# Swapping the issuing engines of two first loads in a convolution with residual

## The chip, the cores and the metric

The kernel runs on one core of one Trainium2 chip. The metric is the device time of one execution in microseconds (us), as the median of several.

## The reference

A 3x3 convolution with zero padding over 16 images of 64 channels, 64 x 64 pixels, to 64 output channels, plus a residual of the output's shape, all in float32:

```python
x_pad = np.pad(x, ((0, 0), (0, 0), (1, 1), (1, 1)))
# for every b, co, ci, kh, kw:
output[b, co] += weight[co, ci, kh, kw] * x_pad[b, ci, kh:kh+64, kw:kw+64]
return output + residual
```

The images, the residual and the output are 16.78 MB each, the weights 0.15 MB: 50.48 MB pass between memory and core.

## The kernel before

Two images make a pair; a pair of images or of residuals is one tile of 128 partitions with rows of 16 KB (2.1 MB). ScalarE casts each image to bfloat16, TensorE (PE) convolves it in 24 matmuls, VectorE (DVE) adds the residual into the tile `ro`, which is then stored. The weights are transposed by PE once and cast by VectorE and ScalarE.

The loads and stores stand in SyncE's program, in order, and so in one queue. Only the first residual load is on ScalarE's queue:

```python
NXR = 3       # image tiles
NXP = 4       # cast images
...
for p in range(NPAIR):                       # on SyncE
    if p >= NXR:
        nc.sync.wait_ge(s_half, 2 * (p - NXR) + 3)     # ScalarE has freed the tile
    if p == 0:
        to_the_front(load_x(p))
        nc.sync.dma_start(out=wraw[:, :], in_=w_rows[:, :]).then_inc(s_w, 16)
    else:
        load_x(p)
    ...                                      # residual loads i = 1..6 follow their pairs
wait_ro(nc.sync, len(RES) - 2)
for pairs in EARLY:                          # stores of pairs 0-1, 2-3, 4-5, 6
    nc.sync.wait_ge(s_add, 2 * pairs.stop + 1)
    store(pairs).then_inc(s_out, 16)
...
to_the_front(load_ro(0, nc.scalar))          # on ScalarE
for n in range(B):
    ...
    if im == 0:
        nc.scalar.wait_ge(s_x[p % NXR], 16 * (p // NXR + 1))
    i = nc.scalar.copy(out=t[64:128, 0:J, :], in_=x4[hp, :, 0, :])
    ...
    if n >= NXP:
        i._wait_ge(s_conv, n - NXP + 1)      # PE has freed the cast image
    ...
    if n == 0:                               # ScalarE's share of the weight casts
        nc.scalar.wait_ge(s_id, NZERO + 1)
```

`to_the_front` moves an issue ahead of everything else that its engine does, so that it goes out within about 0.1 us of the start instead of at about 1 us. The last pair is stored after this program, in two halves.

## Time and profile before

| | before |
|---|---|
| time, median of 3 runs | 122.21 us (122.2 to 122.54) |
| span of the profiled execution | 120.6 us |
| bytes moved | 50.48 MB, 419 GB/s over the span |
| PE, DVE, ACT busy | 73%, 63%, 52% |
| first convolution matmul | 18.12 us |
| VectorE done, last stores issued | 108.6 us, 108.9 and 109.3 us |

### The profile page before, as it was taken

Reading aid. Unit: us, or ns where it says so; the run is one execution under the profiler, and the core shown is the slowest. Engines: PE = TensorE matmul, PEld = TensorE weight load, DVE = VectorE, ACT = ScalarE, POOL = GpSimd, SP = SyncE. Lnnn points to the kernel's source line nnn. Section 1 sums busy time; section 2 is a strip of 40 time slices with the busy share of each in tenths; the row PEclk is TensorE's granted clock in tenths of the full one; section 3 lists DMA queues with packets and bytes.
Section 4 is the critical chain, followed back from the end, with each engine's and each line's share of the span. In section 5 each row is a group of like instructions: output and inputs, shape, how many; then the busy total and the mean of one; then the engine's idle time right before and its main releaser. Section 6 shows DMA issues by size and latency. Waiting matters only on the chain.

```text
span 120.6 us, 734 instructions
## 1 busy us (share of the span) xinstructions
PE 87.7 (73%) x389; PEld 10.7 (9%) x105; DVE 76.0 (63%) x40; ACT 63.1 (52%) x37; POOL 2.4 (2%) x16
## 2 busy tenths in 40 slices
PE   0000609999999999999999999999999999400000
PEld 0000300111101110101010101010101010000000
DVE  0000080039898898988989898898988989890000
ACT  4001999999988595875959578595800000000000
POOL 5200000000000000000000000000000000000000
PEclk9999999999999999999999999999999999995555
DMA  7999999999999999999999999999999999999994
GB/s 239 429 424 429 430 429 429 429 435 435 435 429 429 424 429 424 429 435 424 435 429 435 435 435 418 421 459 435 429 429 429 429 429 435 435 435 429 399 427 168
DMA packets 3808, 50.48 MB, mean 419 GB/s; under 512 B 352, under 2 KB 480, under 8 KB 480
## 3 DMA queue, kind: packets, MB, share of 16 engines
q1 hardware_dynamic: 3664, 48.38, 94.2%
q10 hardware_dynamic: 144, 2.10, 4.1%
HBM read 33.70 MB, written 16.78 MB: 419 GB/s over the span
## 4 chain that ended last, share of the span: by engine, by line
PE 71%; DVEq 2%; DVE 2%; issue 0%
PE ps L101 54%; PE ps L100 17%; DVEq L142 2%; DVE ro L220 2%
## 5 line engine op out<-in xcount | busy, mean ns | idle before, releaser
L220 DVE TENSOR_TENSOR ro<-ps,ro 64x2048 f32<-64x2048 f32 x32 | 73.2, 2288 | 17.7 <-PE ps L101 17.2
L101 PE MATMUL ps<-xp,wl 128*128 128x504 bf16 (+1 forms) x288 | 80.0, 388 | 0.2
L190 ACT CAST xp<-xr 64x2048 bf16<-64x2048 f32 x16 | 30.3, 1896 | 22.5 <-PE ps L101 13.1
L100 PE MATMUL ps<-xp,wl 128*128 128x504 bf16 (+1 forms) x92 | 35.9, 390 | 3.4 <-PEq L241 3.4
L194 ACT CAST xp<-xr 64x2048 bf16<-64x2048 f32 x16 | 30.4, 1898 | 0.4
L100 PEld LDWEIGHTS ps<-xp,wl 128*128 128x128 bf16 x96 | 9.5, 99 | 79.1 <-issue 79.1
L206 DVE CAST wl<-ps 32x192 bf16<-32x192 f32 x8 | 2.8, 348 | 14.9 <-PE ps L233 14.8
L233 PE MATMUL ps<-ident,wraw 128*32 128x128 f32 x9 | 2.1, 412 | 12.6 <-DMA wraw<-in_weight_dram 12.6
L233 PEld LDWEIGHTS ps<-ident,wraw 128*32 128x32 f32 x9 | 1.2, 137 | 13.0 <-issue 12.6
L190 ACT ACT_TABLE_LOAD x1 | 1.3, 1283 | 1.1 <-SPq L142 1.1
L199 ACT CAST wl<-ps 32x192 bf16<-32x192 f32 x4 | 1.2, 306 | 0.0
L177 POOL MEMSET xp<- 64x64 bf16 x4 | 0.6, 146 | 0.2
L176 POOL MEMSET xp<- 64x64 bf16 x4 | 0.6, 144 | 0.2
L165 POOL TENSOR_SCALAR_AFFINE_SELECT ident<-ident 128x128 f32<-128x128 f32 x1 | 0.3, 292 | 0.2 <-POOL ident L163 0.2
L179 POOL MEMSET wl<- 64x192 bf16 x1 | 0.3, 253 | 0.1
L178 POOL MEMSET wl<- 64x192 bf16 x1 | 0.3, 251 | 0.1
L163 POOL MEMSET ident<- 128x128 f32 x1 | 0.2, 204 | 0.7 <-SPq L142 0.7
L277 POOL MEMSET const-bfloat16-1.0<- 128x1 bf16 x1 | 0.1, 111 | 0.0
L277 POOL MEMSET const-uint8-127<- 128x1 uint8 x1 | 0.1, 111 | 0.0
L277 POOL MEMSET const-float32-1.0<- 128x1 f32 x1 | 0.1, 108 | 0.0
L277 POOL MEMSET const-float32-0.0<- 128x1 f32 x1 | 0.1, 103 | 0.2 <-issue 0.2
## 6 DMA issues: line engine op xcount, KB each, us to landing
xr<-in_x_dram SPq DMA_DIRECT2D x8, 2048.0 KB, 14.4
out_dram<-ro SPq DMA_DIRECT2D x3, 4096.0 KB, 19.2
ro<-in_residual_dram SPq DMA_DIRECT2D x2, 4096.0 KB, 20.7
ro<-in_residual_dram SPq DMA_DIRECT2D x2, 2048.0 KB, 18.1
ro<-in_residual_dram ACTq DMA_DIRECT2D x1, 2048.0 KB, 12.0
ro<-in_residual_dram SPq DMA_DIRECT2D x2, 1024.0 KB, 18.8
out_dram<-ro SPq DMA_DIRECT2D x1, 2048.0 KB, 13.7
out_dram<-ro SPq DMA_DIRECT2D x2, 1024.0 KB, 9.4
```

The costliest lines, as they stand in the source:

```text
L100: return e.matmul(out=out_, lhsT=lhsT, rhs=rhs, start=start, stop=stop, skip_group_check=True)
L101: return e.add_instruction(mybir.InstMatmult(name=nc.get_next_instruction_name(), engine=PE, ins=[e.lower_ap(rhs), e.lower_ap(lhsT)], outs ...
L142: with tc.tile_critical(no_gpsimd_drain=True):
L176: nc.gpsimd.memset(t[0:64, 0, :], 0.0).then_inc(s_id, 1)
L177: nc.gpsimd.memset(t[64:128, J, :], 0.0).then_inc(s_id, 1)
L190: i = nc.scalar.copy(out=t[64:128, 0:J, :], in_=x4[hp, :, 0, :])
L194: nc.scalar.copy(out=t[0:64, 1 : J + 1, :], in_=x4[hp, :, 1, :]).then_inc(s_pack, 1)
L199: i = nc.scalar.copy(**weight_block(h, *b))
L206: i = nc.vector.tensor_copy(**weight_block(h, *b))
L220: i = nc.vector.tensor_tensor(out=o4[hp, :, par, :], in0=psj[64 * par : 64 * par + 64, :, :], in1=o4[hp, :, par, :], op=ADD)
L233: i = nc.tensor.transpose(out=tp[0:32, t // 3, 128 * (t % 3) : 128 * (t % 3) + 128], in_=wraw3[:, :, t], identity=ident[:, :])
L277: nc = _bacc.Bacc("TRN2", target_bir_lowering=False, num_devices=1)
```

## The change

The intent: the two first loads go out at the same time on two queues. The change swaps them, so that SyncE's front has the residual and ScalarE's front has the image that ScalarE itself waits for.

```diff
-    def load_x(p):
-        return nc.sync.dma_start(out=xr[p % NXR][:, :], ...
+    def load_x(p, e=nc.sync):
+        return e.dma_start(out=xr[p % NXR][:, :], ...
@@ SyncE
             if p == 0:
-                to_the_front(load_x(p))
+                to_the_front(load_ro(0, nc.sync))
                 nc.sync.dma_start(out=wraw[:, :], in_=w_rows[:, :]).then_inc(s_w, 16)
@@ ScalarE
-        to_the_front(load_ro(0, nc.scalar))
+        to_the_front(load_x(0, nc.scalar))
```

More of the change, by code (lines that the diff above doesn't have):

```diff
@@ L79 @@
     s_add = sem("s_add")
-    def load_x(p):
-        return nc.sync.dma_start(out=xr[p % NXR][:, :], in_=x_bc[128 * p : 128 * p + 128, :]).then_inc(s_x[p % NXR], 16)
+    def load_x(p, e=nc.sync):
+        return e.dma_start(out=xr[p % NXR][:, :], in_=x_bc[128 * p : 128 * p + 128, :]).then_inc(s_x[p % NXR], 16)
     def load_ro(i, e):
```

## The prediction

> **What bounds the kernel now.** I read the page's busy shares by slice first, because the change touches nothing but two loads at the front, and only a kernel that is bound there could feel it.
>
> ```profile
> PE   0000609999999999999999999999999999400000
> DVE  0000080039898898988989898898988989890000
> ACT  4001999999988595875959578595800000000000
> DMA  7999999999999999999999999999999999999994
> GB/s 239 429 424 429 430 429 429 429 435 435 435 429 429 424 429 424 429 435 424 435 429 435 435 435 418 421 459 435 429 429 429 429 429 435 435 435 429 399 427 168
> DMA packets 3808, 50.48 MB, mean 419 GB/s; under 512 B 352, under 2 KB 480, under 8 KB 480
> ```
>
> PE has gaps before its first convolution matmul and is done five slices before the end. The transfers have none: every slice but the first and the last is at 9, at some 430 GB/s. 50.48 MB at 430 GB/s is 117.4 us, and the span is 120.6 us. So the time is the length of one unbroken stream of transfers, plus a start and an end. Two stretches at each end, from the table of stretches (the last column is GB/s), give those:
>
> ```profile
> 0.00:1.00 1.00, 0.00 (x0) 0.00 (x0) 0.00 (x0) 0.00 (x0) 0.21 (x4) 1.00 0.00 0
> 1.00:2.00 1.00, 0.00 (x0) 0.00 (x0) 0.00 (x0) 0.93 (x1) 0.60 (x3) 1.00 1.08 262
> ...
> 118.00:119.00 1.00, 0.00 (x0) 0.00 (x0) 0.00 (x0) 0.00 (x0) 0.00 (x0) 0.50 0.74 311
> 119.00:120.60 1.60, 0.00 (x0) 0.00 (x0) 0.00 (x0) 0.00 (x0) 0.00 (x0) 0.50 0.00 0
> ```
>
> 262/430 of the second microsecond is filled, so data flows from about 1.4 us; 311/430 of the last but one, so it stops at about 118.7. That is 117.3 us of stream, 1.4 us before and 1.9 us after: the 120.6 us. The chain that ended last is put down to PE for 71%, but it is followed from an engine's last instruction at 108.6 us and does not see the queue of stores behind which the last one stands. I set it aside for this reason.
>
> Second, the front, by the timeline (start, length, then the instruction):
>
> ```profile
> 0.00 0.38 SPq L82 DMA_DIRECT2D xr<-in_x_dram  x1
> 0.12 0.36 ACTq L88 DMA_DIRECT2D ro<-in_residual_dram  x1
> 1.11 0.33 SPq L150 DMA_DIRECT2D wraw<-in_weight_dram  x1
> 1.50 0.56 SPq L82 DMA_DIRECT2D xr<-in_x_dram  x1
> ...
> 11.54 1.90 ACT L190 CAST xp<-xr 64x2048 bf16<-64x2048 f32 x1 [9.19 <-DMA xr<-in_x_dram]
> 12.61 2.08 PE L233 MATMUL ps<-ident,wraw 128*32 128x128 f32 x9 [12.61 <-DMA wraw<-in_weight_dram]
> 13.46 1.90 ACT L194 CAST xp<-xr 64x2048 bf16<-64x2048 f32 x1
> 14.80 2.89 DVE L206 CAST wl<-ps 32x192 bf16<-32x192 f32 x8 [14.80 <-PE ps L233]
> 15.27 1.26 ACT L199 CAST wl<-ps 32x192 bf16<-32x192 f32 x4
> ...
> 18.12 0.59 PE L100 MATMUL ps<-xp,wl 128*128 128x512 bf16 x1 [3.44 <-PEq L241]
> ```
>
> The landings of single issues, picked out of the trace by their start: the first image load lands 11.5 us after 0.00, the first residual load 12.0 us after 0.12 (so at 12.1), the weights 11.4 us after 1.11 (at 12.5). The first matmul at 18.12 waits for weights: they land, PE transposes until 14.7, VectorE casts until 14.80 + 2.89 = 17.69. ScalarE's branch, which hangs on the image, ends at 15.27 + 1.26 = 16.53. The image branch has 1.16 us of slack.
>
> **What the Trainium skill says.** "DMA: Bandwidth & Descriptors", section "Queues, rings and completion order": the two issuing engines each own a row of rings on the same 16 transfer engines, and each transfer engine goes round robin between rows, packet by packet. The trace agrees in outline: the two first loads, 4.19 MB together (9.8 us at 430 GB/s), were issued together and landed 0.6 us apart instead of one after the other. The same page, "Issuing engines are not separate DMA queues": issuing from several engines saves only the issue time; here 0.36 to 0.38 us per issue. Section "Where 436 GB/s comes from" gives 435.2 GB/s as the ceiling of the memory's ports; the slices sit at 424 to 435, with single ones at 459 that I take for packets counted at a slice's edge. So there is no rate left to win. "Perfetto Trace Analysis", section "Identifying the Most-Contended Engine", asks for utilization rather than occupancy for transfers, which is why I use GB/s here and not the digit 9.
>
> **The change part by part.** Nothing is added or removed: 2 issues swap queues, everything behind them keeps its place (PE, DVE and POOL have the same instructions; ACT and SP differ in their first one only). Both loads are 2.1 MB in 128 rows of 16 KB, so the bytes and packets on each queue do not change.
>
> 1. Bytes: 50.48 MB before and after. 0 us.
> 2. Start of the stream: one issue at 0.00 on SyncE and one at 0.12 on ScalarE, as before, of the same shape. 0 us, with perhaps 0.1 us of scatter.
> 3. The image load takes the place that the residual load had. By symmetry it lands at about 12.1 instead of 11.5: +0.6 us for ScalarE's first cast, which starts at about 12.15. Its branch then ends at 16.53 + 0.6 = 17.1, still 0.5 us before VectorE's 17.69. The residual lands at about 11.5, and nobody needs it before VectorE's first addition at 26.2.
> 4. The weights stand behind SyncE's first load as before, with as many bytes ahead of them. I leave them at 12.5, and the first convolution matmul at 18.12. 0 us.
> 5. ScalarE's casts of images 0 to 3 run back to back, so they all move by 0.6 us. That moves the issue of the fourth image load, which waits for image 2's first cast, from 22.31 to 22.9. The load ahead of it on SyncE's queue was issued at 2.58 and landed 24.5 us later, at 27.1, so the queue runs dry only some 4.8 us after 22.31, less the 1.4 us from issue to first data seen at the start: 3.4 us of slack against 0.6 used. No gap in the stream. Later casts wait for PE and fall back into step.
>
> Sum on the path that sets the end: 0.0 us.
>
> How much would the end forgive if point 4 is wrong? The last two stores are issued at 108.9 and 109.3, when VectorE has finished. From 109 us on the table of stretches has 451, 426, 385 and 430 GB/s for two microseconds each, then 451 and 311 for one: 0.90 + 0.85 + 0.77 + 0.86 + 0.45 + 0.31 = 4.15 MB. The last two stores are 2.1 MB of these, so 2.05 MB or 4.8 us of older stores stood ahead of them. Less 1.4 us of issue latency, PE and VectorE could be about 3.4 us late (an estimate) before the stream had a hole.
>
> **The rivals.** *The image becomes the bound.* If ScalarE's queue got less than its half, the image would land after 12.66 us (11.5 + 1.16) and move PE's start one for one. For it: that queue's load was already the later one. Against it: it was later by 0.6 us only. Even 2 us late it would stay within the 3.4 us of the end: 122.2 us still. Only if it came after all of SyncE's backlog (four more loads of 2.1 MB or less ahead of it) would it show, at 5 to 10 us; the even sharing seen in the landings speaks against that.
>
> *The weights move.* If the order on the rings is decided by something other than who issues first, the weights could land 0.6 us earlier or later, and PE with them. That too is swallowed at the end: 122.2 us.
>
> *The stream starts later or earlier.* This alone counts one for one. If SyncE's and ScalarE's front issues differ in how soon their data flows, swapping equal shapes still leaves the same pair of starts; I see at most 0.1 to 0.3 us either way, 121.9 to 122.5 us.
>
> *PE is the bound after all*, as the chain has it, and the start of PE sets the end. Then a later image would cost what exceeds its slack, at most a few tenths: 122.2 to 122.6 us. Against it stands the store queue, full at 109 us.
>
> **Range and chances.** All steps sum to nothing, so I take the median of before, 122.21 us, and lean up by a few hundredths because its three runs (122.2, 122.21, 122.54) scatter upward only. 122.25 us. The range is that scatter with the start's 0.3 us: 121.9 to 122.7. 2% would be 2.4 us, which only a hole in the stream or an unfair queue can make: 1% faster, 97% same, 2% slower.
>
> **What would show each step.** After: the slices of transfers at 9 throughout and about 430 GB/s (step 1); data from about 1.4 us (2); ScalarE's first cast at about 12.1 rather than 11.54, still released by the image load (3); the weights' transposes at 12.6 and the first convolution matmul at 18.1, with VectorE's weight casts ending after ScalarE's (4); SyncE's fourth image load issued near 22.9 and the stream without a hole at 25 to 28 us (5). I am wrong if the first cast starts after 12.7 and the last store lands later by the same amount, or if a slice in the middle falls well below 9, or if the stream starts at another time than 1.4 us.

## More of the kernel before

What needs care is the chain of waits. In the page of the kernel before it reads, with shares of the span:

```profile
PE 71%; DVEq 2%; DVE 2%; issue 0%
```

Taken at its word, PE would be the bound. The bandwidth row, shown in the prediction, says something else: the transfers have no gap at all.

## The result, and the profile after

122.35 us (122.34 to 122.52, 4 runs) against 122.37 us of the kernel before (122.2 to 122.54, 4 runs). The ratio is 1.0001, with a 95% interval of 0.9985 to 1.0017: the same. Ratios here are the mean time of one kernel's fast runs over that of the other's of the same rounds, so not quite the ratio of the medians quoted. The output is correct.

The busy tenths and the bandwidth of the kernel after, in 40 slices of its span of 120.5 us:

```profile
PE   0000609999999999999999999999999999300000
DMA  7999999999999999999999999999999999999994
GB/s 228 413 435 434 426 435 430 430 435 430 424 435 435 419 424 435 435 435 435 430 435 435 424 435 413 419 457 435 430 430 435 430 419 435 435 435 419 416 430 188
```

The stream of transfers is as unbroken as before. Its front, by the timeline of the kernel after:

```profile
0.00 0.38 SPq L88 DMA_DIRECT2D ro<-in_residual_dram  x1
0.12 0.36 ACTq L82 DMA_DIRECT2D xr<-in_x_dram  x1
...
12.24 1.90 ACT L190 CAST xp<-xr 64x2048 bf16<-64x2048 f32 x1 [9.89 <-DMA xr<-in_x_dram]
12.67 2.08 PE L233 MATMUL ps<-ident,wraw 128*32 128x128 f32 x9 [12.67 <-DMA wraw<-in_weight_dram]
...
14.86 2.89 DVE L206 CAST wl<-ps 32x192 bf16<-32x192 f32 x8 [14.86 <-PE ps L233]
15.96 1.26 ACT L199 CAST wl<-ps 32x192 bf16<-32x192 f32 x4
...
18.19 0.59 PE L100 MATMUL ps<-xp,wl 128*128 128x512 bf16 x1 [3.44 <-PEq L241]
```

ScalarE's first cast moved from 11.54 to 12.24. Its share of the weight casts now ends at 15.96 + 1.26 = 17.22 instead of 16.53, and VectorE's share still ends last, at 14.86 + 2.89 = 17.75. PE starts its convolutions at 18.19 instead of 18.12.

The landings of the two front issues, before and then after; the row ahead names the issue, the other gives the us to landing:

```profile
L82 SPq DMA_DIRECT2D xr<-in_x_dram x1: 382/382/382, 0.0 to 0.0; - x1
DMA to landing us min/median/max: 11.5/11.5/11.5
...
L88 ACTq DMA_DIRECT2D ro<-in_residual_dram x1: 365/365/365, 0.1 to 0.1; - x1
DMA to landing us min/median/max: 12.0/12.0/12.0
```

```profile
L88 SPq DMA_DIRECT2D ro<-in_residual_dram x1: 383/383/383, 0.0 to 0.0; - x1
DMA to landing us min/median/max: 11.5/11.5/11.5
...
L82 ACTq DMA_DIRECT2D xr<-in_x_dram x1: 364/364/364, 0.1 to 0.1; - x1
DMA to landing us min/median/max: 12.1/12.1/12.1
```

The two tensors changed places, the two landing times stayed. Everything that the change moved is gone again by the end. One difference the change did not make: VectorE's last pair of additions starts at 103.43 instead of 103.99, although PE started 0.07 us later, because PE's first, slower matmuls lasted until about 22.6 instead of 23.6 (the granted clock reads 1.00 from 18 to 24 us in both traces, so the clock row doesn't show it). Kernels with after's front vary as much from one another: these additions start at 103.10 in skip_store and at 104.02 in extra_load, both described below. That VectorE was done 0.56 us sooner and the time stayed the same is already a hint that VectorE and PE don't set the end.

### The profile page after: what moved, and what is told of

The parts are those of the page before. It is cut to its first block, busy times and chain, and to the rows that moved or that the text cites. A ratio compares the mean times of both kernels' runs of the same rounds, so it can differ in the third digit from the quotient of the medians.

```text
span 120.5 us, 734 instructions
## 1 busy us (share of the span) xinstructions
PE 87.1 (72%) x389; PEld 10.7 (9%) x105; DVE 76.0 (63%) x40; ACT 63.1 (52%) x37; POOL 2.4 (2%) x16
## 4 chain that ended last, share of the span: by engine, by line
PE 71%; DVEq 2%; DVE 2%; issue 0%
PE ps L101 53%; PE ps L100 17%; DVEq L142 2%; DVE ro L220 2%
## 5 line engine op out<-in xcount | busy, mean ns | idle before, releaser
L233 PEld LDWEIGHTS ps<-ident,wraw 128*32 128x32 f32 x9 | 1.2, 141 | 13.1 <-issue 12.6
## 6 DMA issues: line engine op xcount, KB each, us to landing
xr<-in_x_dram ACTq DMA_DIRECT2D x1, 2048.0 KB, 12.1
```

The source lines that it names most:

```text
L233: i = nc.tensor.transpose(out=tp[0:32, t // 3, 128 * (t % 3) : 128 * (t % 3) + 128], in_=wraw3[:, :, t], identity=ident[:, :])
```

## The experiments

All start from the kernel after. Each is compared with runs of the kernel before on the same chip (medians of 122.33 to 122.37 us). The theory is the prediction's: an unbroken stream of transfers sets the time, and PE has slack. The main rival is that PE is the bound.

### PE later: pe_late8 and pe_late24

VectorE does idle casts ahead of the weight casts that release PE (8, or 24):

```diff
+        for k in range(8):
+            nc.vector.tensor_copy(out=idle[:, k, :], in_=tp[0:32, 0, 0:384:2])
         for k, b in enumerate(blocks[:4]):
```

> After's kernel, with 8 idle casts of VectorE (0.35 us each, 2.8 us in all) ahead of the weight casts that release PE. Theory (the stream of transfers sets the end, PE and VectorE may be some 3.4 to 4 us late): the first convolution matmul moves from 18.2 to about 21.0, the last stores are issued 2.8 us later, and the time stays at 122.3 to 122.5 us. Rival (the chain that the page shows, PE for 71%, is the bound): 125.1 us.

> The same with 24 idle casts, 8.4 us. Theory: 8.4 us less the 3.4 to 4 us of slack shows, +4.4 to +5.0 us, 126.8 to 127.4 us, with a hole in the stream before the last stores. Rival (PE is the bound): +8.4 us, 130.7 us.

Measured: with 8, 122.38 us (ratio 1.0, 0.9986 to 1.0015). An idle cast added 0.27 us and not 0.35, so PE's first convolution started at 20.16, 2.0 us later than after, and none of it shows. With 24, 124.31 us (123.81 to 124.99; ratio 1.0178, 1.0149 to 1.0207): PE started at 24.44, 6.25 us later, and 1.95 us of it shows in the medians. The rival is out: it wanted the whole delay in both. But the slack is larger than I had said, and the hole is elsewhere. Stretches of pe_late24, the last column is GB/s:

```profile
64.00:65.00 1.00, 1.00 (x6) 0.10 (x1) 1.00 (x1) 0.98 (x2) 0.00 (x0) 1.00 1.10 459
65.00:66.00 1.00, 1.00 (x6) 0.20 (x2) 0.97 (x2) 1.00 (x1) 0.00 (x0) 1.00 1.23 295
66.00:67.00 1.00, 1.00 (x7) 0.10 (x1) 1.00 (x1) 0.66 (x1) 0.00 (x0) 1.00 0.54 147
67.00:68.00 1.00, 1.00 (x6) 0.10 (x1) 0.45 (x1) 0.00 (x0) 0.00 (x0) 1.00 0.81 344
```

The hole lies between loads, at 65 to 68 us: 135 + 283 + 86 GB/s short of 430 over a microsecond each, 504 KB or 1.2 us of stream. The waits of SyncE's queue in 50 to 70 us name its cause (total, times, longest):

```profile
SPq L83 <- ACT xp L191: 19.6, 2, 10.0
```

The seventh and eighth image loads wait for ScalarE to free an image tile, ScalarE waits for PE to free a cast image, and so a late PE makes a late load: the last image load went out at 64.78 instead of 58.7 us. At the end there is no hole of that kind: the last stores were issued at 114.4 and 114.8 and landed 4.2 and 6.3 us later, with one short dip (336 GB/s at 115 to 116 us, 0.2 us of stream). The profiled execution, 123.81 us, is the fastest of the four and 1.45 us slower than before's median, which the hole and this dip make up; what the other three lost more isn't seen in it. So PE may be some 4 to 5 us late before the time grows (an estimate: 6.25 less the 1.95 us of the medians is 4.3, less the 1.2 us of the hole is 5), and in this trace the stream breaks first at the last image load.

### PE earlier: early_pe

```diff
-                to_the_front(load_ro(0, nc.sync))
-                nc.sync.dma_start(out=wraw[:, :], ...)
+                to_the_front(load_x(0))
+                nc.sync.dma_start(out=wraw[:, :], ...)
+                load_ro(0, nc.sync)
 ...
-        to_the_front(load_x(0, nc.scalar))
```

> The first image load alone at SyncE's front, the weights next, the first residual behind them on the same queue, none on ScalarE. The image should land at about 7 us, the weights at about 7.6, the first convolution matmul start some 5 us earlier, at about 13. Theory: bytes and start of the stream are the same, so 122.3 us. Rival (PE is the bound): some 117.5 us. A second rival (one queue alone does not fill the transfer engines): a few tenths slower, and fewer GB/s in the first 12 us.

Measured: 122.76 us (122.65 to 123.03; ratio 1.0038, 1.0025 to 1.0051). The image landed at 7.6, PE started at 13.63, 4.6 us earlier than after, and VectorE's last additions started at 99.64 instead of 103.43. The time did not fall; it rose by 0.4 us. That is the plainest answer to the main rival, and the second rival (one queue alone starts slower) came true. It is taken up under one_queue.

### Fewer and more bytes: skip_store and extra_load

```diff
-    EARLY = (slice(0, 2), slice(2, 4), ...      # skip_store: pair 1 is never stored
+    EARLY = (slice(0, 1), slice(2, 4), ...
```

```diff
+        nc.sync.dma_start(out=spare[:, :], in_=x_bc[0:128, 0:3072]).then_inc(s_e, 16)   # extra_load
         wait_ro(nc.sync, len(RES) - 2)
```

> After's kernel without the store of the second pair of images, 2.1 MB less to write; the output is wrong there on purpose. Theory: the stream is 4.9 us shorter, but the last stores can't be issued earlier than now (108.3), so the time falls by the slack, about 4 us (3.2 to 4.8): 117.6 to 119.2 us. Rival (PE and VectorE are the bound): 122.3 us.

> After's kernel with one more load of 1.57 MB into a spare tensor, behind the last residual load, where nothing that computes waits for it. Theory: +1.57 MB at 430 GB/s = +3.7 us, 126.0 us, with PE and VectorE ending at the same time as in after. Rival (PE and VectorE are the bound): 122.3 us.

Measured: skip_store 117.45 us (117.35 to 118.14), 4.88 us less than before's 122.33, and 2.1 MB at 430 GB/s are 4.88 us. The ratio, 0.9617 (0.9592 to 0.9643), makes it 4.7 us (4.4 to 5.0). Its output is wrong, which doesn't matter for the time. extra_load 126.47 us (126.3 to 126.51; ratio 1.0335, 1.0319 to 1.035), 4.14 us more, where its bytes alone make 3.7; its trace has 382 GB/s at 80 to 84 us, where loads give way to stores, and 446 at 84 to 88 us: a net loss of 0.3 us against 430. In both, PE started at 18.14 to 18.22 us, as in after, and VectorE's last additions at 103.10 and 104.02 us. Bytes that no computing waits for set the time; PE is not the bound.

skip_store also measures the slack of the last stores from the other side. I had expected the saving to stop at 4 us, where these stores could not be issued sooner. They were issued only 0.3 us sooner (108.0 instead of 108.3), and still some 4.7 to 4.9 us were saved. The stretches just before and after the last issues:

```profile
106.00:108.00 2.00, 0.00 (x0) 0.00 (x0) 1.71 (x1) 0.00 (x0) 0.00 (x0) 0.78 1.13 483
108.00:109.00 1.00, 0.00 (x0) 0.00 (x0) 0.00 (x0) 0.00 (x0) 0.00 (x0) 0.50 0.76 328
109.00:110.00 1.00, 0.00 (x0) 0.00 (x0) 0.00 (x0) 0.00 (x0) 0.00 (x0) 0.50 0.98 410
```

There is only a short dip at the issue. What I had too small was the backlog, the older stores that stand ahead of the last two. In after, 417 GB/s over 108.3 to 119 us are 4.46 MB still to start when the last stores go out; less their own 2.10 MB, that is a backlog of 2.36 MB or 5.5 us, where I had reckoned with 4.8 from the trace of before. In skip_store 379 GB/s over 108.0 to 114.4 us are 2.43 MB, so 0.33 MB or 0.8 us of backlog was left. That it hid most of the issue's latency, and that the dip is the rest, fits but is not shown: how long an issue takes to bring data in a running stream no run isolates. The 1.4 us that I took off is not refuted.

### A later start: both_back

Both loads without `to_the_front`.

> After's kernel with both loads issued where the program has them, at 1.1 us, instead of at the engines' front. Theory: the stream starts 1.1 us later and the time follows one for one: 123.4 us. Rival (the start of the stream is hidden as well): 122.3 us.

Measured: 123.64 us (123.29 to 123.75; ratio 1.0095, 1.0081 to 1.011), +1.28 us. They were issued at 0.91 and 0.95 us, not at 1.1. The theory is right that the start counts one for one (0.9 us of it); a third of a microsecond more is unexplained. This is what the front issues are worth, and the swap leaves it alone.

### Which load lands first: sync_back and img_halves

sync_back moves only SyncE's residual load back to where the program has it. img_halves cuts the image load on ScalarE into two loads of 8 KB rows and leaves the residual at 16 KB rows:

```diff
-        to_the_front(load_x(0, nc.scalar))
+        for cols in (RIGHT, LEFT):
+            to_the_front(nc.scalar.dma_start(out=xr[0][:, cols], in_=x_bc[0:128, cols]).then_inc(s_x[0], 16))
```

> After's kernel with only SyncE's residual load moved back from the front to 1.1 us; ScalarE's image load stays at 0.1 us. Theory on time: one queue's load is enough to start the stream, so 122.3 us (rival: two are needed, up to +1.1 us). Theory on the order of landing (who issues first is ahead by one turn of the round robin): the image has the engines to itself for about 1.1 us and lands at about 11.0, a residual later than it. Rival (a load on ScalarE's queue is always the later one): the image stays at 12.1.

> After's kernel with the first image load on ScalarE cut into two loads of 8 KB rows, the residual on SyncE left at 16 KB rows. If the rings are served packet by packet, the residual gets two thirds and lands at about 9.6 instead of 11.5, and the image at about 13.0, which is the end of ScalarE's slack: the first convolution matmul at about 18.5, time still 122.3 us. Rival (served by bytes): 11.5 and 12.1 as in after. Time the same in both.

Measured: sync_back 122.94 us (122.8 to 123.27; ratio 1.0057, 1.0044 to 1.0071). The image, issued first, lands at 10.2 and the residual at 12.6. So ScalarE's queue isn't the later one by nature; the earlier issue is ahead. I had said 11.0, which was too late, and 122.3 us, which was wrong: see one_queue.

img_halves 122.38 us (122.29 to 122.79; ratio 1.0012, 0.9994 to 1.0029). The residual and the two halves of the image, in that order:

```profile
L88 SPq DMA_DIRECT2D ro<-in_residual_dram x1: 383/383/383, 0.0 to 0.0; - x1
DMA to landing us min/median/max: 9.3/9.3/9.3
...
L183 ACTq DMA_DIRECT2D xr<-in_x_dram x2: 376/412/448, 0.1 to 0.5; - x2
DMA to landing us min/median/max: 9.5/11.0/12.5
```

The second half was issued at about 0.5 and landed 12.5 us later, at 13.0; 13.0 was forecast from packets that take turns, where halving one side's rows gives the other side twice its share. By bytes, nothing would have moved. One turn of a 16 KB row on one of 16 transfer engines is 16384 bytes / (430/16 GB/s) = 0.61 us, an estimate from the measured rate, and it fits the 0.6 us between the two landings before and after, as if the load issued 0.12 us later were one turn behind. Here ScalarE's image branch did become PE's last wait: PE's first convolution came at 18.50 instead of 18.19, and the time stayed.

### Why one load at the front costs half a microsecond: one_queue

Both first loads at SyncE's front, at 0.00 and 0.43 us, none on ScalarE.

> Both first loads at SyncE's front, residual first, image second, nothing on ScalarE's queue. It tells why one load alone at the front (early_pe, sync_back) cost 0.4 to 0.6 us. If the engines need two queues to get up to speed, this is slower by the same 0.4 to 0.6 us, 122.8 to 122.9, with fewer GB/s from 1.5 to 2.75 us. If they only need more work issued, 122.35 us, with the GB/s of after. The image lands at about 12 in both.

Measured: 122.89 us (122.8 to 122.93; ratio 1.0044, 1.0029 to 1.0059). The stretch from 1.50 to 2.75 us in after, and then in one_queue:

```profile
1.50:2.75 1.25, 0.00 (x0) 0.00 (x0) 0.00 (x0) 0.85 (x1) 0.93 (x6) 1.00 0.62 249
```

```profile
1.50:2.75 1.25, 0.00 (x0) 0.00 (x0) 0.00 (x0) 1.21 (x1) 0.85 (x5) 1.00 0.47 144
```

249 GB/s with two queues, 144 with one; sync_back has 92 there and early_pe 157. Between after and one_queue that is 131 KB, or 0.3 us of stream; over 0 to 20 us it is 399 against 388 GB/s, some 220 KB or 0.5 us, so the loss lies at the front. (A row is counted where it starts, so short stretches are rough.) The issued work can't be the reason: one_queue had 4.2 MB, 9.8 us of stream, issued by 0.85 us. Two queues at the front start the stream faster than one, and three kernels with one load alone or one queue at the front are 0.4 to 0.6 us slower. What the engines wait for in that stretch no run shows. Both kernels of this case have two queues at the front, so the swap pays nothing here.

### Two attempts to beat both kernels: quarters and mixed

quarters cuts each front load into four with 4 KB rows. mixed has ScalarE issue the first store in the middle of the loads.

> After's kernel with both front loads cut into four of 4 KB rows each, to see whether smaller packets shorten the slow start between 1.5 and 2.75 us that the trace of after also has. If packet size makes it: up to 0.3 us faster, 122.0 to 122.2, the only version tried that could beat both kernels. If not: 122.35, or a few tenths slower for the issues that stand in front of the weights.

> After's kernel with the first 4.2 MB store issued by ScalarE in the middle of the loads instead of by SyncE behind them. Theory (the bytes of one stream set the end, in whatever order they go): 122.35 us. Rival (loads and stores side by side go faster than 430 GB/s, as single slices of 457 to 459 where the stores begin would have it): 459 instead of 430 GB/s over the 19.5 us in which store and loads share, 1.2 us faster, 121.1 us.

Measured: quarters 125.24 us (125.07 to 125.45; ratio 1.0236, 1.0224 to 1.0249), clearly slower. From 3 to 6 us its transfers moved 287, 238 and 336 GB/s while the engines counted as busy throughout (a share of 0.90 to 1.02), and the cut costs 2.9 us instead of winning 0.3. But rows of 4 KB are not slow as such, as two stretches of quarters show:

```profile
3.00:4.00 1.00, 0.00 (x0) 0.00 (x0) 0.00 (x0) 1.00 (x1) 0.66 (x4) 1.00 1.01 287
6.00:8.00 2.00, 0.00 (x0) 0.00 (x0) 0.00 (x0) 0.00 (x0) 0.00 (x0) 1.00 1.02 418
```

From 6 to 8 us the same loads were still under way (ScalarE's first cast, which waits for the image, starts at 14.47), at 418 GB/s. So the loss lies in the first 6 us; whether the short rows there, the eight issues or the slow start itself make it, no run separates. By 20 us quarters is behind after by 1.7 us of stream (363 against 399 GB/s), and its span is 2.2 us longer (122.7 against 120.5); the other 0.7 us of the measured time lie outside the span and stay unexplained.

mixed 123.28 us (123.06 to 123.7; ratio 1.0081, 1.0061 to 1.0102). Around the issue of the store at 49.33 us the stream dips, at 51 to 54 us:

```profile
51.00:52.00 1.00, 1.00 (x6) 0.11 (x2) 0.62 (x1) 0.00 (x0) 0.00 (x0) 1.00 0.91 328
52.00:53.00 1.00, 0.95 (x5) 0.10 (x1) 0.80 (x1) 0.80 (x1) 0.00 (x0) 1.00 1.23 328
53.00:54.00 1.00, 1.00 (x7) 0.10 (x1) 1.00 (x1) 1.00 (x1) 0.00 (x0) 1.00 0.72 262
```

That is 372 KB or 0.9 us lost, and afterwards, where load and store share, it is 434 GB/s (58 to 64 us), not 459. The single slices of 457 and 459 that had tempted me are no higher rate. Why the dip comes, the trace doesn't say. Neither attempt beats the two kernels, and I have found nothing that does: the bytes are fixed, the rate is at 430 GB/s throughout, and the start is already at the front.

## Why the prediction was right

- **What bounds the kernel**: right, and now shown rather than read. 2.1 MB less saved 4.88 us by the medians, 4.88 being what 430 GB/s make of it; PE starting 4.6 us earlier saved nothing; PE 2.0 us later cost nothing. The chain of waits, with PE at 71%, misleads here, as I had argued: it follows instructions and doesn't see the queue of transfers.
- **Step 1, bytes, and step 2, the start**: right. The slices are at 9 throughout. both_back shows that a later start would have counted; the swap makes none. The reading of the start was wrong, though the sum does not suffer: 1.4 us is not when data begins. In quarters of a microsecond the trace of before has rows starting at 655 GB/s from 1.00 to 1.25 us and none from 1.75 to 2.00. So data begins soon after 1 us and comes slowly until some 2.5 us; 1.4 was a mean over both.
- **Step 3, the image**: right. It landed at 12.2 (0.12 + 12.1) for a forecast of 12.1, and the residual at 11.5. "By symmetry" was the right ground, and img_halves fits the reason given: rows take turns, and both loads have rows of one size.
- **Step 4, the weights and PE's start**: right. Weights' transposes at 12.67, PE's first convolution at 18.19, VectorE's casts last by 17.75 - 17.22 = 0.53 us for a forecast of 0.5.
- **Step 5, the fourth image load**: right. It was issued at 23.0 us for a forecast of 22.9, and no slice dips there.
- **The forgiveness of the end, 3.4 us**: the mechanism is right, the size is off, and the place with it. The term mis-sized is the backlog of older stores: 4.8 us reckoned from 109 us in the trace of before, 5.5 us in after at the issue of the last stores. Less 1.4 us that leaves 4.1 us, near the 4 to 5 us that pe_late24 allows. And I looked at the last stores only: pe_late24 shows that a late PE holds up the last image load as well, and there its trace has the hole. Nothing in the forecast of the time hung on it.
- **Rival "the image becomes the bound"**: it did in img_halves, by 0.3 us at PE's start and nothing in the time, as that rival's own figure had it.
- **Point left out**: I took a single queue to be as good as two. That holds in mid-stream and not at the start, where one queue costs 0.4 to 0.6 us. The change keeps two, so the time was right without it.

## What to carry to other kernels

Where the bandwidth row is flat at its ceiling from end to end, ask of a change only whether it alters the bytes, the start of the stream, or leaves a hole in it; order within the stream and a branch with slack cost nothing. Test such a reading by moving bytes that nothing waits for, and by moving the suspected engine both ways. At a program's start, try the first loads on two queues and uncut, which was fastest here; which of two equal loads was on which queue did not matter. And before a later PE or a later store is called harmless, count the backlog at the very issue that it delays.

## What the Trainium skill lacked or had wrong

- "DMA: Bandwidth & Descriptors", section "Issuing engines are not separate DMA queues", says that issuing from several engines only saves issue time. At the program's start the runs show more: two loads on two queues are worth 0.4 to 0.6 us against one queue or one load alone (one_queue 122.89, sync_back 122.94, early_pe 122.76 against 122.33 to 122.37 us), with 249 against 144 GB/s in the stretch from 1.50 to 2.75 us of after and one_queue, although one_queue had 9.8 us of work issued.
- The same page, "Queues, rings and completion order", gives a turn of the round robin as typically 9 to 17 descriptors. Here each first load has 8 rows per transfer engine (128 rows over 16), and the landings fit turns of one row: the two loads landed 0.6 us apart and not one after the other, and halving one side's rows moved the landings from 11.5 and 12.2 to 9.3 and 13.0 us. How many descriptors a row makes no run here shows.
- No page that I consulted states how slowly a program's first transfers come up to speed, or that cutting them can slow them there: quarters, with eight front loads of 4 KB rows, moved 238 to 336 GB/s from 3 to 6 us with the engines counted as busy, then 418 GB/s with the same rows, and took 125.24 us.
